# Three of the four tile pairs of an output projection by seven products, with the two up pairs behind it interleaved

## The chip, the cores and the metric

One core of a Trainium2 chip. The time is device time in microseconds from launch to end, the median of several runs; smaller is better. A profile of one execution stands beside it.

## The reference

One layer on a sequence of 1024 tokens of width 1024, all in float32. Cut to what matters here:

```python
z = rms_norm(h, norm_mix_g)
proj = z @ w_in                                    # 512 pool, 512 recurrent, 512 gate columns
y_pool = multiscale_pool_mixer(u_pool, ...)        # four groups of 128 channels
y_lru = rg_lru(conv(u_lru), ...) * gelu(u_gate)    # four groups of 128 channels
h = h + concatenate([y_pool, y_lru]) @ w_out       # the output projection, 1024 x 1024
z = rms_norm(h, norm_mlp_g)
h = h + square(relu(z @ w_up)) @ w_down            # 1024 -> 4096 -> 1024
h = h + sigmoid(rms_norm(h, norm_ple_g) @ w_ple_gate + b) * (p @ w_ple_proj)
return rms_norm(h, norm_final_g)
```

## The kernel before

Everything is kept with channels on the 128 partitions and the 1024 tokens along the row, so a tensor of width 1024 is eight tiles of 128 x 1024 (`H[0]` to `H[7]` for the residual stream). T[0] to T[5] are six more tiles of that size, R another; A and B are eight pairs each of operand tiles.

A float32 product is made of three products of rounded parts: `split` writes an upper part on ScalarE (a cast) and a lower part on VectorE (source less upper part), and `mm` multiplies upper by upper, upper by lower and lower by upper. Each TensorE instruction multiplies a 128 x 128 block of weights with 512 tokens.

The up and down projections already use seven products for eight (Strassen in Winograd's form): of a 2 x 2 arrangement of blocks, seven products P1 to P7 of sums of operands are made, and their sums give the four corners c11, c12, c21, c22. "Even" and "odd" tiles of a pair and the two halves of the tokens make the operand's 2 x 2; `up_operand` says which operand half each product uses. P1, P2 and P3 use halves as they are (raw), P4 to P7 use sums t1 to t4 made on VectorE. The weights' sums are made partly by accumulating DMAs (`grow`, issued by GpSimd, POOL in the profile), partly on VectorE, in `up_weight`, which also issues the loads of a later pair. An up pair's products can be accumulated onto a PSUM bank that another product or ScalarE wrote before.

The output projection is plain: for each of eight tiles `o`, eight input blocks `k` by three products by two halves of the tokens. `B[0]` to `B[3]` are the pooled channels (`pool_mix`), `B[4]` to `B[7]` the gated recurrent ones (`gate_out`). Of the first two tiles, blocks 0 to 5 come before 6 and 7, since those two are made last. Behind each tile the residual is added on VectorE (line 787), squares are summed for the norm (lines 403 and 404), and after each odd tile the four operand sums for the up projection are made and split into A (line 797 and the two splits behind it). Then `up_first` does the first up pair's seven products in an order of their own, and `up_pair` the others.

The order of the work: the kernel is written as one program, and a planner orders each engine's instructions by readiness and by priority (`tc.high_priority` raises it; `tc.issue_after` and `keep_in_program_order` hold instructions behind others). Each engine and each queue then runs its own list in order. Weights come through `weights()`: it asks for the next entry of the list `todo` and gives out the oldest that was asked for, so weights are split one or two entries ahead. Weight tiles live in four slots (`whi` and `wlo`, two each), raw weights in two (`raw`).

PSUM has eight banks: `pd` gives four single ones (`bank`), `pp` two double ones (`banks`).

Ahead of it all, the first loop (k = 0 to 7) loads the input tiles with the first weights on SP's queue and multiplies as they come; GpSimd computes a small series there (`softplus`, lines 498 to 509), whose result `cneg` and `cpos` the recurrence uses later (line 665).

## Time and profile before

| | us |
|---|---|
| median of 3 runs (918.67 to 919.38) | 919.19 |
| the profiled execution | 918.4 |
| its span, first to last instruction | 916.6 |
| TensorE busy in the span | 909.1 |
| VectorE busy | 703.8 |
| ScalarE busy | 468.6 |
| GpSimd busy | 38.9 |
| output projection on TensorE, 384 instructions | 82.88 |
| first up pair on TensorE, 84 instructions | 18.13 |

PE is TensorE's multiplication, PEld its weight load, DVE VectorE, ACT ScalarE, POOL GpSimd, SP the queue of plain loads and stores. A row of the timeline has its start, its length, engine, line, operation, what it writes and reads, and, in square brackets, how long the engine was idle before it and what ended that. Tile names leave out buffer numbers: `t_h` are the T and H tiles, `a` the A tiles, `y` the B tiles, `wu` and `wu_raw` raw up weights, `ps_o` the projection's banks.

### The profile page before, as it was taken

To read this page: it belongs to the slowest core of one execution; us is meant where nothing else is said; L and a number is where in the kernel's file an instruction comes from. 1 tells how busy PE (TensorE), PEld (TensorE's weight loads), DVE (VectorE), ACT (ScalarE), POOL (GpSimd) and SP (SyncE) were. 2 spreads that over 40 slices of the span, in tenths; PEclk is the share of its full clock that TensorE was granted. 3 is DMA by queue.
4 is the path that set the end of the run, shared out by engine and by line. 5 is a ranking of instruction groups with operands and counts; after the bars stand their busy time and mean duration, and the time that the engine had idled before them with its cause. 6 is when DMAs were issued, how large, how long until landed. Compare 5 with 4: busy or idle time off the path is not lost.

```text
span 916.6 us, 11225 instructions
## 1 busy us (share of the span) xinstructions
PE 909.1 (99%) x4225; PEld 792.0 (86%) x4225; DVE 703.8 (77%) x854; ACT 468.6 (51%) x606; POOL 38.9 (4%) x54
## 2 busy tenths in 40 slices
PE   9999999999999999999999999999999999999997
PEld 7888888888888888888888888888888888888886
DVE  7898984668986566656765899899876579799676
ACT  6558992447554454445444554344343446656223
POOL 4400001000000000000000000000000000000001
PEclk9999999999999999999999999999999999999999
DMA  7311055214377767876864987466633341031353
GB/s 274 102 46 46 24 182 140 81 46 117 103 209 224 210 163 217 227 197 169 231 206 164 353 335 276 131 195 203 201 117 117 115 162 46 1 119 67 92 174 136
DMA packets 56871, 142.46 MB, mean 155 GB/s; under 512 B 4977, under 2 KB 9969, under 8 KB 56817
## 3 DMA queue, kind: packets, MB, share of 16 engines
q1 hardware_dynamic: 54080, 132.84, 43.7%
q0 software_dynamic: 2736, 8.91, 5.7%
q8 instruction: 33, 0.54, 0.3%
q14 instruction: 22, 0.17, 0.1%
HBM read 106.08 MB, written 35.65 MB: 155 GB/s over the span
## 4 chain that ended last, share of the span: by engine, by line
PE 98%; issue 1%; DVE 0%; DVEq 0%; ACT 0%; POOLq 0%; POOL 0%
PE ps_P_d L363 32%; PE ps_b_u L363 12%; PE ps_i L363 9%; PE ps_o L363 9%; PE ps_d_u L363 8%; PE ps_a_u L363 8%; PE ps_e L363 8%; PE ps_l L363 3%; PE ps_P_u L363 3%; PE ps_e L1254 2%; PE ps_l L576 1%; PE ps_j L363 1%; PE ps_g L645 1%; PE ps_p L363 1%; PE ps_l_second L363 1%
## 5 line engine op out<-in xcount | busy, mean ns | idle before, releaser
L363 PE MATMUL ps_P_d<-a,wd_P_hi 128*128 128x512 f32 x880 | 261.7, 379 | 0.0
L363 PEld LDWEIGHTS ps_P_d<-a,wd_P_hi 128*128 128x128 f32 x880 | 166.3, 189 | 23.6
L363 PE MATMUL ps_P_d<-a,wd_P_lo 128*128 128x512 f32 x440 | 166.8, 379 | 0.0
L363 PE MATMUL ps_b_u<-a,wu_P 128*128 128x512 f32 x504 | 113.5, 379 | 0.0
L363 PEld LDWEIGHTS ps_b_u<-a,wu_P 128*128 128x128 f32 x504 | 95.3, 189 | 13.5
L363 PEld LDWEIGHTS ps_P_d<-a,wd_P_lo 128*128 128x128 f32 x440 | 83.2, 189 | 11.8
L363 PE MATMUL ps_a_u<-y,wu_P 128*128 128x512 f32 x360 | 82.6, 379 | 0.0
L363 PEld LDWEIGHTS ps_a_u<-y,wu_P 128*128 128x128 f32 x360 | 68.0, 189 | 9.7
L826 DVE TENSOR_TENSOR t_h<-t_h,ps_P_d 128x512 f32<-128x512 f32 (+1 forms) x56 | 42.5, 759 | 36.2 <-PE ps_P_d L363 36.2
L186 DVE TENSOR_TENSOR a<-wd,a 128x1024 fp32r<-128x1024 f32 x56 | 67.0, 1219 | 0.9 <-ACT a L185 0.6
L363 PE MATMUL ps_i<-a,wi_hi 128*128 128x512 f32 x256 | 66.1, 381 | 0.0
L363 PE MATMUL ps_o<-y,wo_hi 128*128 128x512 f32 x256 | 65.7, 379 | 0.0
L185 ACT ACTIVATE a<-wd 128x1024 fp32r<-128x1024 f32 x56 | 57.9, 1049 | 7.0 <-PE ps_P_d L363 7.0
L363 PEld LDWEIGHTS ps_i<-a,wi_hi 128*128 128x128 f32 x256 | 48.1, 189 | 8.0 <-issue 0.7
L363 PEld LDWEIGHTS ps_o<-y,wo_hi 128*128 128x128 f32 x256 | 48.4, 189 | 6.9
L185 ACT ACTIVATE wd_P_hi<-wd 128x1024 fp32r<-128x1024 f32 x24 | 25.3, 1055 | 56.0 <-PE ps_P_d L363 56.0
L844 DVE SCALAR_TENSOR_TENSOR t_h<-t_h,rstd 128x2048 f32<-128x2048 f32 x16 | 36.6, 2291 | 18.8 <-ACT t_h L863 18.8
L186 DVE TENSOR_TENSOR wu_P<-wu,wu_P 128x512 fp32r<-128x512 f32 x47 | 32.2, 687 | 21.8 <-ACT wu_P L185 21.8
L186 DVE TENSOR_TENSOR wu_P<-wu_raw,wu_P 128x512 fp32r<-128x512 f32 x45 | 30.9, 687 | 23.3 <-ACT wu_P L185 23.3
L363 PE MATMUL ps_d_u<-a,wu_P 128*128 128x512 f32 x180 | 41.3, 379 | 0.0
L363 PE MATMUL ps_d_u<-y,wu_P 128*128 128x512 f32 x180 | 41.3, 379 | 0.0
L185 ACT ACTIVATE wu_P<-wu 128x512 fp32r<-128x512 f32 x47 | 29.3, 625 | 21.1 <-PE ps_b_u L363 14.0
(267 smaller groups left out, 1545.7 us busy)
## 6 DMA issues: line engine op xcount, KB each, us to landing
wd<-act SPq DMA_DIRECT2D x56, 512.0 KB, 5.5
act<-t_h SPq DMA_DIRECT2D x32, 512.0 KB, 6.2
wu<-in_w_up SPq DMA_DIRECT2D x16, 512.0 KB, 4.7
act<-wu SPq DMA_DIRECT2D x16, 512.0 KB, 5.9
wd<-in_w_down SPq DMA_DIRECT2D x16, 512.0 KB, 5.8
wu_raw<-in_w_up SPq DMA_DIRECT2D x15, 512.0 KB, 5.5
t_h<-in_xT SPq DMA_DIRECT2D x14, 512.0 KB, 4.8
wg_raw<-in_w_gate SPq DMA_DIRECT2D x10, 512.0 KB, 3.3
```

The costliest lines, as they stand in the source:

```text
L185: first = pin(nc.scalar.activation(hi, src, AF.Copy))
L186: lowest[:] = [pin((eng or nc.vector).tensor_tensor(lo, src, f32(hi), ALU.subtract)).ins]
L363: ins = nc.tensor.matmul(ps, w, turns(z[:, hs]), start=first and z is zhi and w is whi, stop=last and w is wlo, skip_group_check=more,)
L576: nc.tensor.matmul(ps, kblk(w, o), turns(z[:, hs]), start=k == n == 0, stop=False)
L645: nc.tensor.matmul(x, w[r, o * P : (o + 1) * P], turns(z[r, at : at + HALF]), start=n == 0, stop=n == 2)
L826: (eng or nc.vector).tensor_tensor(to, to if y is None else y, x, ALU.add)
L844: nc.vector.scalar_tensor_tensor(cc, cc, 0.0, twice(R), ALU.max, ALU.mult)
L1254: nc.tensor.matmul(pg, z, turns(quad[x == 1][:, k]), start=n == 0, stop=n == 3 * NT - 1, skip_group_check=True)
```

## The change

The first two output tiles stay plain. The other three pairs (numbered -3, -2, -1 in the list of weights) are made by seven products each (`out_pair`), from operand sums of the mixed channels. `out_sums` makes these sums in place, in the tiles that hold the mixed channels, and splits them into A; to keep the tiles until then, the fourth gated tile goes to `H[6]`, two pooled tiles to `H[4]` and `H[5]`, and the other two are stored to HBM (`mixed`) and loaded back. The three raw products of a pair come first. P3's weight is the sum of all four blocks; for the three out pairs and the first two up pairs it is made in HBM by `sum_ahead`, called in the first loop: for each of five sums one copy and three accumulating transfers of 256 KB by GpSimd's queue. The corners of the first two such pairs are written over H, and the residual is added to them by an accumulating load; the last pair's are added to a residual loaded before.

The double PSUM banks are given up after the plain pair for four single ones (`part_upper`). The up operands' sums are in place too (`up_sums`, `up_even`, `up_odd`). The first two up pairs are interleaved (`up_two`), raw products first, with the norm's sums folded between them. In the last up pair P4 moves ahead of P2. The down stage keeps its products.

```diff
-    pp = ctx.enter_context(tc.tile_pool(name="pp", bufs=2, space=bass.MemoryType.PSUM))
     pd = ctx.enter_context(tc.tile_pool(name="pd", bufs=4, space=bass.MemoryType.PSUM))
+    upper_half = [ExitStack()]
+    pp = upper_half[0].enter_context(tc.tile_pool(name="pp", bufs=2, space=bass.MemoryType.PSUM))
+    pe = []
+    def part_upper():
+        upper_half[0].close()
+        pe.append(ctx.enter_context(tc.tile_pool(name="pe", bufs=4, space=bass.MemoryType.PSUM, reuse_waits="tile")))
...
+    def pair_source(m):
+        return w_up[m] if m >= 0 else w_pairs[m + NOUT]
+    def load_a22(m):
+        nc.sync.dma_start(up_raw[m]["P4"], pair_source(m)[:, A22])
+    full_sums = {m: dram.tile([P, HALF], F32, name=f"full{m}") for m in range(-NOUT, 2)}
+    out_raw = []
+    def sum_ahead():
+        for m, to in full_sums.items():
+            w = pair_source(m)
+            nc.gpsimd.dma_start(to, w[:, A21])
+            for x in (A22, A11, A12):
+                grow(to, w[:, x])
+    def load_pair(m):
+        w = pair_source(m)
+        a, c = (H[7], T[4]) if m == -2 else [raw_tile(f"wu{m}_{i}") for i in range(2)] if m % 2 else up_spare
+        (a11, a12), (chain, s3) = halved(a), halved(c)
+        a22, full = T[5][:, HALVES[m % 2]], chain if m < NPAIR - 1 else T[4][:, FIRST]
+        if m < 2:
+            few = {-3: out_raw[0], -2: R, -1: T[5]}.get(m, out_raw[1])
+            full = few[:, HALVES[int(m == 1)]]
+            if m < 0:
+                a22 = few[:, SECOND]
+        up_raw[m] = {"P1": a11, "P2": a12, "P4": a22, "P5": chain, "P6": chain, "P7": s3, "P3": full}
         nc.sync.dma_start(a, w[:, A11.start : A12.stop])
         if m < 2:
+            nc.sync.dma_start(full, full_sums[m])
             load_a22(m)
+        nc.sync.dma_start(both(c), twice(w[:, A21]))
+        grow(c, w[:, : 2 * HALF])
...
+    RAW_FIRST = "P1", "P3", "P2", "P5", "P6", "P4", "P7"
+    UP = [(m, kind) for m in range(-NOUT, 0) for kind in RAW_FIRST]
+    UP += [(m, kind) for kind in RAW_FIRST[:3] for m in TWO]
+    UP += [(0, "P5"), (0, "P6"), (1, "P5"), (0, "P7"), (1, "P6"), (0, "P4"), (1, "P7")]
+    for m in range(2, NPAIR - 1):
+        UP += [(m, "P1"), (m, "P5"), (m - 1, "P4"), (m, "P6"), (m, "P2"), (m, "P3"), (m, "P7")]
     m = NPAIR - 1
+    UP += [(m, "P1"), (m, "P5"), (m - 1, "P4"), (m, "P4"), (m, "P2"), (m, "P3"), (m, "P6"), (m, "P7")]
     def up_weight(m, kind):
+        raw, last = up_raw[m], m == NPAIR - 1
         w = wp.tile([P, S], F32R, tag=next(up_place), name=f"wu{m}_{kind}")
         hi, lo = (w[:, hs] for hs in HALVES)
+        with tc.high_priority(URGENT) if m < 0 else ExitStack():
+            split(raw[kind], hi, lo)
+            if kind == "P5":
+                dv(ALU.add, raw["P5"], raw["P5"], raw["P1"])
+                if last:
+                    dv(ALU.add, raw["P3"], raw["P6"], raw["P2"])
+            elif kind == "P6" and 2 <= m < NPAIR - 1:
+                dv(ALU.add, raw["P3"], raw["P6"], raw["P2"])
+        if kind == "P7" and m < NPAIR - 2 and m != -2:
+            load_pair(m + 2)
+        if kind == "P4" and 0 <= m < NPAIR - 2:
+            load_a22(m + 2)
         return hi, lo
...
         if k == 3:
             tables()
+            sum_ahead()
...
-    GATED = T[5], T[1], T[0], T[1]
+    GATED = T[5], T[1], T[0], H[6]
+    MIXED = T[5], T[2], H[4], H[5]
...
+            if pair == 0:
+                nc.sync.dma_start(mixed[:, t], y)
...
-    out_w, out_ps = {}, {}
-    for o in range(NT):
-        nc.sync.dma_start(H[o], xT[o * P : (o + 1) * P, :])
-        if o == 0:
-            out_w = {0: weights(), 1: asked.pop(0)}
-            seed_up()
-            for i in range(2):
-                out_ps[i] = psum(f"ps_o{i}")
-                out_parts(i, out_w[i], out_ps[i], range(NT - 2))
-        elif o == 1:
-            ask()
-        else:
-            out_w[o], out_ps[o] = weights(), psum(f"ps_o{o}")
-        out_parts(o, out_w[o], out_ps[o], range(NT - 2, NT) if o < 2 else range(NT))
-        ps = out_ps[o]
-        z = T[o % 2]
-        end = o == NT - 1
-        for hs, part in ps:
-            hv = by(H[o][:, hs], part)
-            nc.vector.tensor_tensor(hv, hv, got(part), ALU.add)
-            if end:
-                nc.scalar.activation(z[:, hs], H[o][:, hs], AF.Identity, scale=col("g_mlp", o))
-        if not end:
-            norm.add(H[o])
-            nc.scalar.activation(z, H[o], AF.Identity, scale=col("g_mlp", o))
-        if o % 2 == 1:
-            z11, z12, z21, z22 = (T[i][:, hs] for i in range(2) for hs in HALVES)
-            t2, t3, t4, t1 = (T[i][:, hs] for i in (2, 3) for hs in HALVES)
-            for to, x, y in ((t1, z11, z12), (t2, z22, t1), (t3, z12, z22), (t4, z21, t2)):
-                nc.vector.tensor_tensor(to, x, y, ALU.add if to is t2 else ALU.subtract)
-            split(T[2], *A[o // 2])
-            split(T[3], *A[4 + o // 2])
...
+    def out_operand(kind, t):
+        if kind in ("P5", "P7"):
+            return half(A[t], int(kind == "P7"))
+        if kind in ("P4", "P6"):
+            return half(A[4 + t], int(kind == "P6"))
+        return half(B[2 * t + (kind != "P1")], int(kind == "P3"))
...
+        if t == 3 and kind in ("P1", "P2", "P3", "P4"):
+            return half(A[3 + int(kind[1])], 0)
+        if kind == "P4":
+            return half(B[2 * t], 1)
+        return out_operand(kind, t)
...
+    def seed(b, a):
+        nc.scalar.activation(b, a, AF.Copy, scale=-1.0)
+    def sums(even, odd):
+        (z11, z12), (z21, z22) = halved(even), halved(odd)
+        dv(ALU.subtract, z11, z11, z12)
+        dv(ALU.subtract, z12, z12, z22)
+        dv(ALU.add, z22, z22, z11)
+        dv(ALU.subtract, z21, z21, z22)
+    def out_sums(t, even, odd):
+        sums(even, odd)
+        split(even, *A[t])
+        split(odd, *A[4 + t])
+    def residual(o):
+        return xT[o * P : (o + 1) * P, :]
+    def first_out(i):
+        ps = out_ps[i]
+        for hs, part in ps:
+            add_got(H[i][:, hs], part)
+    for o in range(2):
+        nc.sync.dma_start(H[o], residual(o))
+    out_w = [weights(), asked.pop(0)]
+    leave("hl")
+    out_raw += space("hr", 2, F32, waits="tile")
+    load_pair(-NOUT)
+    load_pair(-2)
+    out_ps = [[(slice(0, S), banks(f"ps_o{i}"))] for i in range(2)]
+    for ks in (range(NT - 2), range(NT - 2, NT)):
+        for i in range(2):
+            out_parts(i, out_w[i], out_ps[i], ks)
+    for _ in range(2):
+        ask()
+    for t in range(2):
+        nc.sync.dma_start(T[2 + t], mixed[:, t])
+    out_sums(2, T[5], T[1])
+    out_sums(1, H[4], H[5])
+    out_sums(0, T[2], T[3])
+    with tc.high_priority(URGENT):
+        for i in range(2):
+            first_out(i)
+    part_upper()
+    out_sums(3, T[0], H[6])
+    def corners(q):
+        return [H[2 * q + i][:, hs] for i in range(2) for hs in HALVES]
+    def out_pair(q, end=False):
+        m = q - 1 - NOUT
+        c11, c12, c21, c22 = corners(q)
+        keep = add_got if end else copy
+        a, d = bank(f"ps_a_o{q}"), bank(f"ps_d_o{q}")
+        b, f = upper_bank(f"ps_b_o{q}"), upper_bank(f"ps_f_o{q}")
+        pair_product(m, "P1", a)
+        seed(b, a)
+        pair_product(m, "P3", d)
+        keep(c22, d)
+        pair_product(m, "P2", a, more=True)
+        keep(c11, a)
+        yield "raw"
+        pair_product(m, "P5", d, more=True)
+        if end:
+            add_got(c12, d)
+        pair_product(m, "P6", b, more=True)
+        if end:
+            less(c12, b)
+        else:
+            copy(c12, b)
+            take(c12, d, c12)
+        pair_product(m, "P4", f)
+        keep(c21, f)
+        yield "fourth"
+        pair_product(m, "P7", b, more=True)
+        add_both(both(H[2 * q + 1]), b)
+        less(c22, d)
+        if not end:
+            for o in (2 * q, 2 * q + 1):
+                grow(H[o], residual(o))
+    def up_raw_part(t, kinds):
+        for kind in kinds:
+            o = 2 * t + (kind != "P1")
+            split(H[o][:, HALVES[kind == "P3"]], *up_operand(kind, t), col("g_mlp", o))
+    def up_sums(t, even, odd):
+        for i, z in enumerate((even, odd)):
+            nc.scalar.activation(z, H[2 * t + i], AF.Identity, scale=col("g_mlp", 2 * t + i))
+        sums(even, odd)
+    def up_odd(t, odd):
+        split(odd[:, FIRST], *up_operand("P4", t))
+        split(odd[:, SECOND], *up_operand("P6", t))
+    def up_even(t, even):
+        split(even, *A[t])
+    for q in (1, 2):
+        for _ in out_pair(q):
+            pass
+        up_sums(q - 1, T[2 * q - 2], T[2 * q - 1])
+    norm = Norm("n1", R, T[4:5])
+    for o in range(4):
+        norm.add(H[o])
+    for o in (6, 7):
+        nc.sync.dma_start(H[o], residual(o))
+    stages = out_pair(3, True)
+    next(stages)
+    leave("y2")
+    *E, u0, u1 = space("wu", 4, F32, "right", "tile")
+    up_spare += u0, u1
+    load_pair(0)
+    for t in range(3):
+        up_raw_part(t, RAW_FIRST[:3])
+    next(stages)
+    up_raw_part(3, RAW_FIRST[:1])
+    up_sums(2, *E)
+    for _ in stages:
+        pass
+    up_raw_part(3, RAW_FIRST[1:3])
+    for t in range(2):
+        up_even(t, T[2 * t])
+        up_odd(t, T[2 * t + 1])
+    up_sums(3, T[0], T[1])
+    up_even(2, E[0])
+    up_odd(2, E[1])
+    up_even(3, T[0])
+    up_odd(3, T[1])
+    for o in range(4, NT):
+        norm.add(H[o])
...
+    def up_two():
+        (a, d), (b, f) = ([[new(f"ps_{x}_u{m}") for m in TWO] for x in xs] for new, xs in ((bank, "ad"), (upper_bank, "bf")))
+        cc = [corner_sums(m)[1:] for m in TWO]
+        for m in TWO:
+            pair_product(m, "P1", a[m])
+            seed(b[m], a[m])
+        for m in TWO:
+            pair_product(m, "P3", d[m])
+        for m in TWO:
+            pair_product(m, "P2", a[m], more=True)
+            copy(cc[m][0], a[m])
+        leave("hr")
+        small[:] = space("hl", 2, F32R, waits="tile")
+        for hs in HALVES:
+            norm.fold(hs, T[4][:, hs])
+        def fifth(m):
+            pair_product(m, "P5", f[m])
+            copy(cc[m][3], f[m])
+        def sixth(m):
+            c12 = cc[m][1]
+            pair_product(m, "P6", b[m], more=True)
+            copy(c12, b[m])
+            take(c12, d[m], c12)
+            add_got(c12, f[m])
+        def seventh(m):
+            pair_product(m, "P7", b[m], more=True)
+            take(cc[m][3], b[m], cc[m][3])
+        fifth(0)
+        sixth(0)
+        norm.rstd(R, [x for hs in HALVES for x in norm.folded(hs)])
+        fifth(1)
+        seventh(0)
+        sixth(1)
+        chains[0] = b[0]
+        up_fourth(0)()
+        seventh(1)
+        chains[1] = b[1]
+        leave("hl")
...
+        ps = mlp_bank(f"ps_P4_u{m}")
+        pair_product(m, "P4", ps)
+        copy(c21, ps)
...
+        W[0, 3] = raw_tile("w11_3")
+        load_w(0, 0, 3)
...
-            ps = banks(f"ps_e{g}_{o}")
-            pair = ps[:, :HALF], ps[:, HALF:]
+            pair = upper_bank(f"ps_e{g}_{o}"), upper_bank(f"ps_j{g}_{o}")
...
+    wo = np.asarray(w_out)[0].reshape(NT // 2, 2, P, NT // 2, 2, P).transpose(3, 4, 1, 2, 0, 5)
+    wo = np.stack([wo[1:, i, j] for i, j in ((1, 1), (0, 0), (0, 1), (1, 0))], axis=2)
```

210 lines of the change are left out of this document (59 added, 151 removed).

## The prediction

> **What bounds the kernel now.** I read the page first, then the chain of waits in order of time.
>
> ```profile
> span 916.6 us, 11225 instructions
> PE 909.1 (99%) x4225; PEld 792.0 (86%) x4225; DVE 703.8 (77%) x854; ACT 468.6 (51%) x606; POOL 38.9 (4%) x54
> PE 98%; issue 1%; DVE 0%; DVEq 0%; ACT 0%; POOLq 0%; POOL 0%
> ```
>
> ```profile
> 120.99 20.72 PE ps_i L363 x96
> 141.71 82.88 PE ps_o L363 x384
> 224.59 18.13 PE ps_P_u L363 x84
> 242.72 2.59 PE ps_a_u L363 x12
> ```
>
> TensorE is the chain. Each piece begins where the last one ended (141.71 + 82.88 = 224.59), so there is no gap around the change: whatever removes a matmul is gained whole, and whatever makes TensorE wait is lost whole. So the next question is what cover the other engines have. The view by stretches gives it; its columns are the stretch and its length, then busy time of PE, PEld, DVE, ACT, POOL, the granted clock, DMA share and GB/s.
>
> ```profile
> 2.00:16.00 14.00, 14.00 (x60) 10.85 (x59) 10.47 (x22) 8.65 (x17) 2.70 (x7) 1.00 0.95 337
> 121.00:141.70 20.70, 20.70 (x97) 18.12 (x97) 19.81 (x18) 16.21 (x17) 0.00 (x0) 1.00 0.55 200
> 141.70:159.90 18.20, 18.20 (x87) 15.92 (x86) 6.02 (x7) 4.38 (x5) 2.74 (x3) 1.00 0.61 149
> 141.70:253.10 111.40, 111.40 (x518) 97.55 (x517) 77.57 (x101) 56.20 (x71) 5.43 (x6) 1.00 0.36 96
> ```
>
> VectorE is full ahead of the output projection (19.81 of 20.70), two thirds idle in its first 18.2 us (6.02), and has 77.57 of 111.4 over the stretch that the new projection and the first two up pairs will fill.
>
> **The change part by part.**
>
> *Matmuls.* One matmul is 82.88 / 384 = 0.2158 us. A pair of output tiles takes 96 now (two tiles, eight blocks, three products, two halves) and 7 × 4 × 3 = 84 by seven products. Three pairs: 36 fewer, **-7.77 us**. The up pairs keep 84 each (18.13 us), the down stage keeps its count. TensorE would then have the plain pair from 141.71 to 162.43, three raw products to 170.2, the third pair's end at 216.8 and two up pairs to 253.1, if nothing waits.
>
> *VectorE's prices.* The nearest rows, from the timeline:
>
> ```profile
> 159.87 1.22 DVE L787 TENSOR_TENSOR t_h<-t_h,ps_o 128x1024 f32<-128x1024 f32 x1 [10.11 <-PE ps_o L363]
> 166.48 1.89 DVE L797 TENSOR_TENSOR t_h<-t_h 128x512 f32<-128x512 f32 x3
> 168.89 2.36 DVE L186 TENSOR_TENSOR a<-t_h,a 128x1024 fp32r<-128x1024 f32 x2 [0.52 <-ACT a L185]
> 218.94 6.04 DVE L189 SCALAR_TENSOR_TENSOR y<-t_h,y 128x512 fp32r<-128x512 f32 x9
> 238.15 1.29 DVE L445 TENSOR_TENSOR t_h<-t_h 64x512 f32<-64x512 f32 x2
> 239.36 0.94 DVE L448 CAST hl<-t_h 64x512 fp32r<-64x512 f32 x2
> 240.34 1.59 DVE L449 TENSOR_TENSOR hl<-t_h,hl 64x512 fp32r<-64x512 f32 x2
> 250.01 1.31 DVE L465 STREAM_TRANSPOSE rstd<-n_ps 128x512 f32<-128x512 f32 x2
> 252.04 0.47 DVE L470 RECIPROCAL edge<-edge 128x16 f32<-128x16 f32 x2
> 252.43 1.24 DVE L471 STREAM_TRANSPOSE rstd<-edge 128x512 f32<-128x512 f32 x2
> 254.16 2.28 DVE L844 SCALAR_TENSOR_TENSOR t_h<-t_h,rstd 128x2048 f32<-128x2048 f32 x1
> ```
>
> So a half row (512) is 0.63, a full row (1024) 1.18, a scaled half 0.67.
>
> *New sums before the projection (out_sums).* Four calls of four half sums and two full lower parts: 4 × (2.52 + 2.36) = 19.5 us on VectorE, none there before. They are due at the first product that isn't raw: P5 of the first pair, 170.2, its fourth block at 172.1; the last lower part (1.18) only in P6. By 159.9 VectorE has 18.2 - 6.0 = 12.2 us for them. From there to 172.1 it must also do first_out (2 × 1.18), five lower weight halves and one chain sum (6 × 0.63), 6.2 in all, which leaves 6.0. Due 18.3, room 18.2: the margin is nil. Lower bound 0. Upper bound: only the long idle piece of 10.11 is used and each call waits 0.52 for ScalarE, so 2.1 + 2.1 = 4.2. I take **+0.5**, near the lower end, since the P4 weight can slip behind them.
>
> *Weight halves, and how far ahead.* Each out weight is now a half tile in one of four slots. The first needs the slot of the first plain tile.
>
> ```profile
> 159.49 1.06 ACT L185 ACTIVATE wo_hi<-wo_raw 128x1024 fp32r<-128x1024 f32 x1 [10.99 <-PE ps_o L363]
> 213.83 0.63 ACT L185 ACTIVATE wu_P<-rstd 128x512 fp32r<-128x512 f32 x1 [3.21 <-PE ps_o L363]
> 245.34 0.58 ACT L926 ACTIVATE ps_b_u<-ps_a_u 128x512 f32<-128x512 f32 x1 [0.23 <-PE ps_a_u L363]
> ```
>
> The kernel before makes the same jump with a whole tile (1.06 + 1.22 from 159.49, used at 162.43) and TensorE doesn't wait; half tiles need 0.63 + 0.63. Cost 0, covered by the plain pair's last 2.6 us. ScalarE's new work (21 half casts less 6 whole, 8 whole casts for the sums, some 13 PSUM copies and seeds at 0.58) is about 23 us, 79 of 111.4: no bound.
>
> *The rest of the stretch.* VectorE from 141.7 to 253.1: what stays of the recurrence 6.0; out_sums 19.5; first_out 2.4; 21 weight halves and 3 chain sums 15.1; the pairs' corners 2 × 2.44 + 4.96 = 9.9; the up operands 10.1 + 4.7 + 5.0 + 8.0 = 27.8; the norm 7 × 1.18 + 3.8 + 3.0 = 15.1; two up pairs 22 × 0.63 = 13.9; the first finish_up 4.7. Sum 114.4 against 111.4 us. So VectorE goes from 70% to full. But norm and finish_up (19.8) don't feed the next products: they may slide behind 253, where a pair leaves it slack, and 94.6 fit. What is late next is the norm's two small matmuls, which the code puts after eight of the two up pairs' fourteen products, at 237.5. Bounds 0 and 4 (3.0 us of excess and the 1.2 of a full row ahead of it); I take **+0.2**.
>
> *Loads that are moved.* The accumulating loads of each pair go out on POOL (0.86 each) behind all that stands there before.
>
> ```profile
> 0.72 0.10 POOL L502 MEMSET sp<- 128x4 f32 x1 [0.29 <-POOLq L1493]
> 3.75 0.24 POOL L513 TENSOR_TENSOR sp<-t_h 128x4 f32<-128x4 f32 x1 [2.93 <-DMA t_h<-in_w_vec_x]
> 12.91 0.24 POOL L498 TENSOR_SCALAR sp<-sp 128x4 f32<-128x4 f32 x1 [8.93 <-ACT sp L497]
> 32.41 1.83 POOL L509 TENSOR_SCALAR sp<-sp 128x4 f32<-128x4 f32 x1
> 159.13 0.86 POOL L227 DMA_DIRECT2D rstd<-in_w_up x1 [5.19 <-DMA rstd<-in_w_up]
> ```
>
> ```profile
> q0 software_dynamic: 432, 0.79, 31.6%
> ...
> rstd<-in_w_up POOLq DMA_DIRECT2D x3, 256.0 KB, 5.0
> ```
>
> The second fence is the DMA view from 150 to 166 us: three accumulating transfers of 256 KB, 5.0 us each to land, 31.6% of 16 us, so 1.69 us of all DMA engines each. sum_ahead adds 20 of that size (5 copies, 15 that accumulate) from HBM to HBM; each sum waits for the one before, so POOL is held about 5.9 us a step, up to 118 us. The first pair's own chain is needed at 170 and would be free of this at about 150.
>
> Where they start matters more. The planner puts on POOL what is ready: L502 and L513 ran ahead of L498, which precedes them in the code. The twenty transfers wait for nothing, so they may begin at about 1 us, in the stretch where the DMA engines are full (0.95 from 2 to 16 us). The tightest load there:
>
> ```profile
> 15.42 1.15 ACT L188 ACTIVATE a<-t_h 128x1024 fp32r<-128x1024 f32 x1 [0.19 <-DMA t_h<-in_xT]
> 17.09 1.20 DVE L189 SCALAR_TENSOR_TENSOR a<-t_h,a 128x1024 fp32r<-128x1024 f32 x1
> 21.25 1.03 PE L363 MATMUL ps_l<-a,wl_hi 128*128 128x512 f32 x4
> ```
>
> The fifth input tile lands at 15.4, its lower part is done at 18.3, TensorE needs it at 21.25: 2.96 us to spare. One transfer at a time takes 1.69 of 5.9 us, 29% of the DMA engines; the loads from 2 to 15.4 then stretch by 1/0.71, 5.4 late, and TensorE waits 2.4. With half of the engines taken they are 13.4 late and it waits 10.4. With a later start it is 0. Bounds 0 and 10.4; I take **+1.0**, between none and one at a time.
>
> [...]
>
> *At no cost:* storing and reloading two pooled tiles (512 KB each; due at 160, DMA share 0.61 then), the residual by accumulating loads (two for each of two pairs, due only when the up operands are made, a pair later), four single PSUM banks in place of two pairs, and the new order in the last up pair. Each has a whole pair (18.1 us) or the idle half of the DMA engines as cover; without it a late load costs its 5 to 8 us.
>
> *Sum.* 918.4 (the profiled execution) - 7.77 + 0.5 + 0.2 + 1.0 = 912.3. The median of the runs stands 0.8 above the profiled execution, so **913.1**.
>
> **The rivals.**
>
> *VectorE becomes the bound at the sums.* For it: margin nil at 172.1, 114.4 us of work in 111.4. Against: a sixth of that can slide. Price 4.2 + 4 at most, half of it likely: one wait of about 4 us, 915.6. [...]
>
> *The start slowed a little:* one transfer at a time throughout, 2.4 in place of 1.0, with the small waits 914.5.
>
> *Slower: the ahead-sums flood the start.* Place: 2 to 16 us, DMA queues. Price by the share taken: a half gives 10.4 of waiting against 7.77, 918.4 + 2.6 + 0.8 = 921.8. It decides from 45% on (10.7 late = 7.77 + 2.96, over 13.4 + 10.7). For it: five of the twenty don't depend on each other and could be in flight together; the engines are full then. Against: POOL waits in order for each sum. The same queue also holds the softplus steps, done at 34.2 and used at 82.5; eight of the twenty put ahead of them (8 × 5.9) use that room up.
>
> *The products aren't removed,* or come back elsewhere: the counts of the code say no; I give it nothing.
>
> **How the numbers follow.** Forecast (911.2 to 914) 0.53; VectorE the bound 0.16; start a little slowed 0.17; flooded start 0.12; POOL's softplus late 0.02. Faster or slower by 0.2% means below 917.4 or above 921.0, about what a measurement of this kernel can tell from no change. The forecast lies below; of the VectorE case 0.14 does, of the small start case 0.13 (more than one transfer at a time for the rest); 0.05 of the flooded start stays within, 0.07 and the softplus case lie above. So faster 0.80, same 0.11, slower 0.09. The range runs from all terms at 0 (911.4, less 0.4 of scatter) to 918.5, which leaves out the flooded start and the worst of the others.
>
> **What would show it.** 36 fewer matmuls, the projection's four pieces 20.7 and three times 18.1 us. A wait of TensorE on a lower part of "a" near 172 is the sums' price, one ahead of the norm's small matmuls near 240 the slide's; TensorE idle before 36 us with ScalarE waiting for x is the start's, with POOL's transfers issued in the first microseconds. The prediction is wrong if TensorE waits somewhere not named here, or if its pieces aren't 0.2158 us a matmul.

## The result, and the profile after

The changed kernel takes 949.93 us (median of 4 runs, 947.08 to 952.24); the kernel before took 919.10 beside it. The ratio is 1.0334, with a 95% interval of 1.0306 to 1.0363: 31 us slower, where 6 us faster was forecast. The profiled execution took 952.24 us, with a span of 950.5 beside 916.6.

The page of the changed kernel, its first lines and its chain by engine:

```profile
span 950.5 us, 11308 instructions
PE 914.9 (96%) x4189; PEld 790.4 (83%) x4189; DVE 732.7 (77%) x900; ACT 490.7 (52%) x646; POOL 51.8 (5%) x78
PE 71%; DVE 15%; DMA 7%; ACT 3%; issue 3%; SPq 0%; DVEq 0%; POOLq 0%; POOL 0%; ACTq 0%
```

The 36 matmuls are gone (4225 to 4189). Yet TensorE, which was 98% of the chain, is 71% of it, and it is busy for longer. At the mean of before (909.1 / 4225), 4189 matmuls last 901.3 us, so 13.6 us of the 914.9 are matmuls that ran slowly. Idle time went from 7.5 to 35.6 us, 28.1 more. The sum is 28.1 + 13.6 - 7.8 = 33.9, the difference of the spans.

Where it is lost shows in the pieces of TensorE. The timeline of the changed kernel, at the start of the projection, the three places where it stood still longest behind it, and the first up product:

```profile
153.11 1.03 PE L384 MATMUL ps_o<-y,wo_hi 128*128 128x512 f32 x4
...
178.89 5.49 PE L384 MATMUL ps_a_o<-y,wu-3_P 128*128 128x512 f32 x12 [4.54 <-ACT wu-3_P L196]
...
207.57 4.38 PE L384 MATMUL ps_a_o<-y,wu-2_P 128*128 128x512 f32 x12 [2.18 <-ACT ps_b_o L843]
...
244.01 2.11 PE L384 MATMUL ps_a_u<-y,wu_P 128*128 128x512 f32 x9
...
260.27 3.28 PE L384 MATMUL ps_d_u<-y,wu_P 128*128 128x512 f32 x7 [5.83 <-DVE wu_P L197]
```

The projection starts 11.4 us late (153.11 where before had 141.71, both by the same product). It lasts 90.9 us to the first up product, where 384 less 36 matmuls would be 75.1: 15.8 lost. From there to the end of P6 of the third up pair, the seventeenth up product in both kernels, before needed 44.5 us (224.59 to 269.05) and the changed kernel 57.4 (244.01 to 301.36): 12.9 lost. The chain of waits has the product behind these two ends, first of the kernel before, then of the changed one:

```profile
269.05 2.59 PE ps_a_u L363 x12
```

```profile
301.36 2.59 PE ps_a_u L384 x12
```

The rest adds 1.6. So these three stretches lose 40 us, of which the removed matmuls pay for 7.8. The view of stretches of the changed kernel, with the columns of the prediction:

```profile
2.00:16.00 14.00, 9.70 (x33) 6.69 (x32) 6.04 (x13) 2.90 (x9) 3.58 (x7) 0.88 0.97 302
150.00:170.00 20.00, 19.92 (x93) 17.13 (x92) 20.00 (x24) 10.44 (x11) 1.76 (x2) 1.00 0.60 166
178.00:185.00 7.00, 6.11 (x15) 4.87 (x16) 6.43 (x10) 5.18 (x9) 0.00 (x0) 0.51 0.22 75
240.00:260.00 20.00, 10.88 (x44) 8.20 (x44) 20.00 (x28) 14.65 (x22) 1.73 (x2) 0.83 0.32 62
```

*The start.* From 2 to 16 us TensorE has 9.70 of 14.00 where it had 14.00. The timeline of POOL in the changed kernel, and the DMA view of its first 50 us:

```profile
1.30 0.75 POOL L261 DMA_DIRECT2D full-3_136<-in_w_pairs  x1 [0.47 <-issue]
2.03 0.58 POOL L261 DMA_DIRECT2D full-2_137<-in_w_pairs  x1
2.58 0.54 POOL L261 DMA_DIRECT2D full-1_138<-in_w_pairs  x1
3.10 0.54 POOL L261 DMA_DIRECT2D full<-in_w_up  x1
```

```profile
q0 software_dynamic: 2128, 4.46, 46.5%
q1 hardware_dynamic: 3227, 7.76, 45.9%
...
t_h<-in_xT SPq DMA_DIRECT2D x6, 512.0 KB, 10.2
```

Four of the five copies go out together in the first four microseconds. GpSimd's queue q0 takes 46.5% of the DMA engines, and the input tiles land 10.2 us after their issue. The same view of the kernel before has no q0 and 5.8 us:

```profile
q1 hardware_dynamic: 3456, 8.56, 49.4%
...
t_h<-in_xT SPq DMA_DIRECT2D x6, 512.0 KB, 5.8
```

*The projection's start.* Behind the wait of 4.54 us stand twelve matmuls that took 5.49 us in place of 2.59, and the stretch from 178 to 185 has a granted clock of 0.51. What the wait is for is in the timeline of ScalarE:

```profile
177.25 1.06 ACT L196 ACTIVATE a<-t_h 128x1024 fp32r<-128x1024 f32 x1 [2.48 <-DVE t_h L229]
178.22 0.61 ACT L196 ACTIVATE wu-3_P<-wu-3_0_raw 128x512 fp32r<-128x512 f32 x1
...
205.88 1.15 ACT L933 ACTIVATE t_h<-t_h 128x1024 f32<-128x1024 f32 x1 [5.00 <-DMA t_h<-in_xT]
206.94 0.58 ACT L843 ACTIVATE ps_b_o<-ps_a_o 128x512 f32<-128x512 f32 x1
```

The cast of the first weight, 0.61 us, stands on ScalarE behind a cast of `out_sums` that had waited 2.48 us for VectorE, which is full there (20.00 of 20 us from 150 to 170). No raw product needs that sum.

*The second pair.* In the same fence a scaling of the up sums waits 5.00 us for the accumulating residual load, and the seed of the next pair's chain (ScalarE's copy of that pair's first product, with its sign turned, into the bank that later products are added onto) stands behind it. That is the wait of 2.18 us at 207.57. One pair later a square of the norm waits 3.37 us for such a load, again ahead of the seed, and TensorE waits 1.68.

*The up pairs' start.* TensorE waits from 254.4 to 260.27 for a lower part, one of the two in the second row of this fence from VectorE's timeline:

```profile
255.45 0.70 DVE L229 TENSOR_TENSOR t_h<-t_h 128x512 f32<-128x512 f32 x1
...
259.52 1.30 DVE L197 TENSOR_TENSOR wu_P<-hr,wu_P 128x512 fp32r<-128x512 f32 x2
```

VectorE does not rest from 240 to 260 (20.00 of 20). Ahead of the two subtractions of 0.65 us stand an addition of the norm and operand sums such as the first row's and their lower parts, which the first product of sums (ps_f_u, at 270.68 in the chain of waits) needs 10 us later.

### The profile page after: what moved, and what is told of

Same layout as the page of the kernel before. It is cut to its first block, busy times and chain, and to the rows that moved or that the text cites. A ratio compares the mean times of both kernels' runs of the same rounds, so it can differ in the third digit from the quotient of the medians.

```text
span 950.5 us, 11308 instructions
## 1 busy us (share of the span) xinstructions
PE 914.9 (96%) x4189; PEld 790.4 (83%) x4189; DVE 732.7 (77%) x900; ACT 490.7 (52%) x646; POOL 51.8 (5%) x78
## 4 chain that ended last, share of the span: by engine, by line
PE 71%; DVE 15%; DMA 7%; ACT 3%; issue 3%; SPq 0%; DVEq 0%; POOLq 0%; POOL 0%; ACTq 0%
PE ps_P_d L384 31%; PE ps_b_u L384 11%; PE ps_d_u L384 8%; PE ps_a_u L384 8%; PE ps_e L384 7%; DMA t_h<-in_xT 3%; PE ps_e L1379 2%; PE ps_j L384 2%; DVE t_h L229 2%; DMA wu<-in_w_up 1%; DVE a L197 1%; DVE t_h L640 1%; DVE y L197 1%; DVE t_h L627 1%; DMA wl_raw<-in_w_lru 1%
## 5 line engine op out<-in xcount | busy, mean ns | idle before, releaser
L384 PE MATMUL ps_b_u<-a,wu_P 128*128 128x512 f32 x405 | 92.3, 379 | 0.0
L384 PEld LDWEIGHTS ps_b_u<-a,wu_P 128*128 128x128 f32 x405 | 76.5, 189 | 10.9
L384 PE MATMUL ps_a_u<-y,wu_P 128*128 128x512 f32 x288 | 68.3, 382 | 2.0 <-ACT wu_P L196 2.0
L384 PEld LDWEIGHTS ps_a_u<-y,wu_P 128*128 128x128 f32 x288 | 54.5, 190 | 10.2 <-ACT wu_P L196 2.6
L229 DVE TENSOR_TENSOR t_h<-t_h 128x512 f32<-128x512 f32 x46 | 31.5, 690 | 33.8 <-ACT t_h L991 23.6
L384 PE MATMUL ps_d_u<-a,wu_P 128*128 128x512 f32 x216 | 51.5, 379 | 0.0
L384 PEld LDWEIGHTS ps_d_u<-a,wu_P 128*128 128x128 f32 x216 | 41.0, 190 | 5.9
L384 PE MATMUL ps_d_u<-y,wu_P 128*128 128x512 f32 x144 | 35.7, 393 | 6.1 <-DVE wu_P L197 5.8
```

The source lines that it names most:

```text
L229: return nc.vector.tensor_tensor(to, x, y, op).ins
L384: ins = nc.tensor.matmul(ps, w, turns(z[:, hs]), start=first and z is zhi and w is whi, stop=last and w is wlo, skip_group_check=more,)
```

## The experiments

Differences below are of medians; each kernel also has its ratio to the kernel before, with its 95% interval.

**The twenty transfers alone, in the kernel before.**

```diff
+    full_sums = {m: dram.tile([P, HALF], F32, name=f"full{m}") for m in range(5)}
+    def sum_ahead():
+        for m, to in full_sums.items():
+            nc.gpsimd.dma_start(to, w_up[m][:, A21])
+            for x in (A22, A11, A12):
+                grow(to, w_up[m][:, x])
...
+            sum_ahead()
```

> The kernel before with only the twenty ahead-sum transfers added (same size, same sources of 256 KB, into buffers that nothing reads), called at the same place of the first loop; the computation is unchanged. Theory 'flooded start': between before and after, the first input-gate product ps_i starts at 46.88 and at 58.29 us, 11.4 us later, and the twenty transfers alone make this. Expected: 930.5 us (919.1 + 11.4), ps_i near 58, GpSimd's softplus ending near 50 in place of 34. Rival 'the start is late for another reason' (other weights' layout, the planner's other choices): within 2 us of 919.1 and ps_i near 47.

Measured: 928.35 us, ratio 1.0103 (1.0088 to 1.0118). The chain of waits of this kernel:

```profile
2.11 8.81 DMA wl_raw<-in_w_lru
...
55.66 10.36 PE ps_i L372 x48
```

The first gate product starts at 55.66 where before had 46.88, 8.8 late. So the transfers alone cost 9.2 us; the flooded start is shown. The changed kernel's 11.4 has 2 us more, and no run parts those.

**The transfers held behind the softplus series**, in the changed kernel.

```diff
+        series_end.append(nc.gpsimd.tensor_scalar_mul(cneg, cpos, -1.0).ins)
...
-            sum_ahead()
+            with tc.issue_after(series_end[0]):
+                sum_ahead()
```

> The changed kernel with the twenty ahead-sum transfers held behind the last step of the softplus series on GpSimd (done near 34 us when it is undisturbed), same computation. Theory 'flooded start': TensorE gets back the 11.4 us of the start and the rest is as in after: 949.9 - 11.4 = 938.5 us, ps_i starts near 47. Rival: the transfers only move their harm, for they are then in the way of the loads from 34 to 110 us: between 940 and 950, with new waits of TensorE on casts of loaded tiles in that stretch.

Measured: 940.67, ratio 1.0235 (1.0220 to 1.0250): 9.3 us back, 2.1 less than expected. TensorE is busy for all of 2 to 36 us again, and its first gate product starts at 47.05 in the timeline (46.72 before). The time itself lies in the rival's range (940 to 950), but its sign is missing: TensorE waits nowhere from 34 to 110 us. The 2.1 us are lost later, where the waits for seeds grew from 3.9 to 5.4 us in all and the one for a lower part from 5.8 to 6.4. The next ones build on this kernel.

**ScalarE's scalings behind the next pair's fourth product.**

```diff
+        with tc.issue_after(marks["fourth", q]):
             up_sums(q - 1, T[2 * q - 2], T[2 * q - 1])
...
+    with tc.issue_after(marks["fourth", 2]):
         for o in range(4):
             norm.add(H[o])
```

> As the one with the ahead-sums held back, and beside it ScalarE's scalings of the up sums (which wait for the accumulating residual transfers, 5.00 and 3.37 us of ScalarE standing still in after) are put behind the next pair's fourth product's copy, and with them the squares of the norm; the computation is the same. Theory 'order on ScalarE': the seeds of the second and third output pair no longer stand behind them, so the waits ahead of wu-2 (2.18 us and 1.79 of half clock) and wu-1 (1.68) go, about 5 us: near 933.5 beside 938.5. Rival 'VectorE is the bound': it is 100% busy from 150 to 170 and from 240 to 260 us in after, and work put later only adds to the second stretch: within 1.5 us of the kernel it is made from, or slower.

Measured: 938.35, ratio 1.0209 (1.0192 to 1.0226), 2.3 us back in place of 5. The waits of TensorE in this kernel (us in total, times, longest) begin with

```profile
PE ps_d_u L384 <- DVE wu_P L197: 10.9, 1, 10.9
PE ps_a_o L384 <- ACT wu-3_P L196: 4.5, 1, 4.5
```

The run also holds the casts of raw operands of the first up products, and the norm's last squares, behind the third pair's seed. Both waits for seeds are gone, and half of what they gave is lost again at the up pairs' start, where the wait for a lower part grew from 6.4 to 10.9 us. Each theory has half of it.

**The last call of `out_sums` behind the first weight.**

```diff
-    out_sums(3, T[0], H[6])
+    with tc.issue_after(first_up), tc.issue_after(first_low):
+        out_sums(3, T[0], H[6])
```

> As the one with the ahead-sums held back, and beside it the last of the four calls that make the projection's operand sums is held behind the first product's weight parts (both its upper part on ScalarE and its lower part on VectorE); the computation is the same. Theory 'order on ScalarE': in after wu-3_P's cast (178.22, 0.61) stood behind casts of sums (2.48 us of waiting for VectorE) that the raw products don't need; with fewer of them ahead, the wait of 4.54 us and the 2.9 us of half clock behind it (twelve matmuls in 5.49 in place of 2.59) shrink by 2 to 7 us: 931 to 936 beside 938.5. Rival 'VectorE is the bound': the sums come later by what the weights come earlier, TensorE waits for the last sum's lower part at the first product of sums in place of it, and the time stays within 1.5 us.

Measured: 936.81, ratio 1.0195 (1.0180 to 1.0210), 3.9 us back: within the 2 to 7 us of "order", though not within its 931 to 936, which counted from 938.5 in place of 940.67. The timeline has, in place of a wait of 4.54 and a halved clock:

```profile
165.40 2.43 PE L384 MATMUL ps_a_o<-y,wu-3_P 128*128 128x512 f32 x10 [1.71 <-DVE wu-3_P L197]
```

**High priority for the first up pairs' weights.**

```diff
-        with tc.high_priority(URGENT) if m < 0 else ExitStack():
+        with tc.high_priority(URGENT) if m < 2 else ExitStack():
```

> As the kernel with the ahead-sums held back (940.7), and beside it the planner's high priority for weight parts, which the output pairs have, is given to the first two up pairs too; the computation is the same. In that kernel TensorE waits 6.4 us for the lower part of an up weight on VectorE, which stands behind some 20 us of operand sums that only later products need, and 2.0 for an upper part on ScalarE; twenty matmuls behind the wait take 6.56 us in place of 4.32. Theory 'order on VectorE': the weights' lower parts (0.68 each) go ahead, the waits fall to 2 us in all: 931 to 934. Rival 'VectorE is too full there (18.84 of 20 us from 240 to 260)': the operands of the later products become late by the same amount, and TensorE waits for a lower part of them instead: within 2 of 940.7.

Measured: 933.98, ratio 1.0160 (1.0141 to 1.0179), 6.7 us back. The wait of 6.4 us for a lower part of an up weight is gone from the list, and 1.2 us at the norm's small matmuls is the longest wait left at the up pairs. The operand sums that stood ahead were not needed yet: order, not the amount of work, made this wait.

**The three changes of order at once.**

> The ahead-sums held back, and all three changes of order at once: ScalarE's scalings behind the fourth product's copy (alone 940.7 to 938.4), the last operand sum behind the first weight (to 936.8), the up weights at high priority. The computation is the same. Theory 'order': the gains are at different places and add: -2.3 - 3.9 - 8 = 926.5, slower than before by 7 us, since the accumulating residual loads (7 us to land) stay. Rival 'VectorE is the bound over the whole of the stretch': the stretch has about 114 us of its work in 104, and whatever is moved shows up as a wait elsewhere: not below 933.

Measured: 927.86, ratio 1.0092 (1.0077 to 1.0107). Together they give 12.8 us, the sum of the three (2.3 + 3.9 + 6.7 = 12.9), as "order" had it; the rival's 933 is passed. The longest waits left are 3.2 us for a seed and 1.9 for an operand's lower part, both at the up pairs.

**The residual loaded first**, with the last sum behind the first weight and the weights at high priority, without the held scalings.

```diff
     for q in (1, 2):
-        for _ in out_pair(q):
+        for o in (2 * q, 2 * q + 1):
+            nc.sync.dma_start(H[o], residual(o))
+        for _ in out_pair(q, True):
             pass
```

> The ahead-sums held back, the last operand sum behind the first weight, the up weights at high priority, and the residual of the second and third output pair loaded on SP ahead of their products and added to the PSUM parts on VectorE (as the last pair does), in place of copies on ScalarE and four accumulating transfers afterwards. The result is the same sum. Theory 'late residual': the seeds no longer stand behind scalings that wait for a transfer (4.06 and 1.35 us of waiting in the kernel with the sums ordered, and 1.9 of half clock behind the first): 936.8 - 8 (weights) - 7.3 = 921.5, though VectorE has 4 x 0.68 more for each pair. Rival 'VectorE is the bound': those 5.4 us come on top: 930 or more, the waits on lower parts grow.

Measured: 920.66, ratio 1.0019 (1.0009 to 1.0028). It has VectorE do more (735.0 us by its page, 732.7 in the changed kernel) and is 7.2 us faster than the three orders, near the forecast of "late residual" (921.5). It differs from them in three things: no accumulating transfers, eight corner copies fewer on ScalarE, and nothing held. Against the two orders that it keeps, which would give 930.1 if their gains add (an estimate: 940.67 - 3.9 - 6.7), it gives 9.4. So making the residual late cost 7 to 9 us; how much of that is the transfers and how much the copies no run parts.

**Operand sums early, their parts behind the first weight.**

```diff
-    out_sums(0, T[2], T[3])
+    sums(T[2], T[3])
...
+    sums(T[0], H[6])
+    with tc.issue_after(first_up), tc.issue_after(first_low):
+        for t, even, odd in ((0, T[2], T[3]), (3, T[0], H[6])):
+            split(even, *A[t])
+            split(odd, *A[4 + t])
```

> As the one with the residual loaded first, but of the projection's operand sums two calls are parted: the sums themselves are made as early as before, only their upper and lower parts are held behind the first weight of the projection. Same computation. Theory 'order on ScalarE': the cast of the first weight no longer waits for VectorE's sums (in the kernel with one call held it starts at 162.26, behind a cast that waited 2.41 us, and TensorE waits 1.71 us): 1 to 2 us less than the one it is made from. Rival: the lower parts that were moved are due at the first product of sums (ps_d_o at 172.8) and are late there by what the weights gained: no difference, within 0.7.

Measured: 920.16, ratio 1.0016 (1.0007 to 1.0026): 0.5 less, which these runs can't tell from none, as the rival had it. The waits of TensorE in this kernel and three of its stretches:

```profile
PE ps_d_o L384 <- DVE t_h L823: 1.2, 1, 1.2
PE n_ps L478 <- DVE hl L470: 1.2, 1, 1.2
PE ps_P_d L384 <- ACT a L196: 1.1, 1, 1.1
PE ps_a_o L384 <- DVE wu-3_P L197: 0.9, 1, 0.9
```

```profile
133.00:150.00 17.00, 17.00 (x81) 14.88 (x80) 17.00 (x19) 10.61 (x12) 0.90 (x1) 1.00 0.76 221
150.00:160.00 10.00, 9.95 (x47) 8.39 (x46) 10.00 (x13) 3.71 (x5) 0.86 (x1) 1.00 0.83 256
220.00:240.00 20.00, 19.39 (x89) 16.35 (x88) 20.00 (x29) 14.37 (x23) 0.00 (x0) 1.00 0.37 81
```

What is left are waits of about 1 us, three of the four for VectorE, which is full in all three stretches; the waits come behind them (163 to 174, and 253 us). The granted clock is 1.00 again.

**The old order of the last up pair, three fine changes of order, and both.** The first puts P4 of the last pair behind P2 and P3 again, in the list of weights and in `up_last`; the second has three edits:

```diff
-    UP += [(m, "P1"), (m, "P5"), (m - 1, "P4"), (m, "P4"), (m, "P2"), (m, "P3"), (m, "P6"), (m, "P7")]
+    UP += [(m, "P1"), (m, "P5"), (m - 1, "P4"), (m, "P2"), (m, "P3"), (m, "P4"), (m, "P6"), (m, "P7")]
```

```diff
-    with tc.high_priority(URGENT):
+    with tc.high_priority(URGENT), tc.issue_after(first_low):
         for i in range(2):
             first_out(i)
...
-        keep(c22, d)
+        with tc.high_priority(URGENT):
+            keep(c22, d)
...
-        norm.rstd(R, [x for hs in HALVES for x in norm.folded(hs)])
         fifth(1)
         seventh(0)
+        norm.rstd(R, [x for hs in HALVES for x in norm.folded(hs)])
```

> As the kernel whose operand sums are parted (920.2), and beside it the last up pair's products stand in the order of the kernel before again (P2 and P3 ahead of its own P4). The computation is the same. In that kernel the first down products wait 1.07 us for an upper part and 0.56 for a lower part; the chain of waits shows a load of 5.93 us into the tiles of the raw operands, released by the last raw product at 508.72. Theory 'the new order of the last pair delays the loads': two raw products one product earlier (2.59 us) take both waits away: -1.6, 918.5. Rival 'the order costs nothing': within 0.5.

> As the kernel whose operand sums are parted (920.2), and beside it three small changes of order: the first pair's residual additions go behind the first weight's lower part (TensorE waits 0.89 us there), the copy of the corner that P5 accumulates onto goes at high priority (1.20), and the norm's two small matmuls go behind two more products (1.16). The computation is the same. Theory 'order': 3.2 us in all, 917.0. Rival 'VectorE is full' (20.00 of 20 us from 220 to 240): the waits move to other lower parts and half or less is gained: 918.5 or more.

> The three small changes of order and the old order of the last pair together; the computation is the same. If both theories hold: 920.2 - 1.6 - 3.2 = 915.4, faster than before (919.0) by 3.6. If VectorE is the bound in the stretch: 917 to 918.5.

Measured: 920.74, ratio 1.0022 (1.0013 to 1.0032), for the last pair; 919.36, ratio 1.0005 (0.9996 to 1.0014), for the fine order; 919.25, ratio 1.0009 (1.0000 to 1.0017), for both. The old order of the last pair gains nothing (0.6 us slower than without it): that rival holds. The two together miss both of their forecasts (915.4, and 917 to 918.5). Of the fine order's 3.2 us no more than 0.8 came, and the waits of TensorE in that kernel show how:

```profile
PE ps_a_o L384 <- ACT ps_b_o L846: 1.3, 1, 1.3
PE n_ps L478 <- DVE hl L470: 1.2, 1, 1.2
```

The waits of 0.9 and 1.2 at the first pair are gone, and one of 1.3 for its seed stands there. The norm's matmuls wait as before: the planner did not move them with the code.

**GpSimd takes work from VectorE**: the norm's last four additions, the four sums of the pooled tiles, or both.

```diff
+    norm.eng = nc.gpsimd
     for o in range(4, NT):
         norm.add(H[o])
...
-    sums(T[2], T[3])
+    sums(T[2], T[3], nc.gpsimd)
```

> As the kernel with the three fine changes of order (919.4), and the last four additions of the norm's squares (128 x 1024, 1.22 us each on VectorE) are made on GpSimd; the computation is the same. No row shows such an addition on GpSimd, which stands idle there. Theory 'VectorE is what is left of the loss': VectorE has 4.9 us less from 239 to 250, and the waits there (0.60 for a lower part, 1.16 for the norm's small matmuls, 0.24 for a subtraction) shrink: 917.5 to 918.5 if GpSimd needs less than 2.5 us each. Rival 'GpSimd is slower than VectorE there, and its time stands on the path of the norm': TensorE waits longer for the small matmuls, 921 or more.

> As the kernel with the three fine changes of order (919.4), and the four half sums of the two pooled tiles ahead of the projection (128 x 512, 0.68 us each on VectorE) are made on GpSimd; the computation is the same. Theory 'VectorE is what is left of the loss': it is busy 17 of 17 us from 133 to 150 and 10 of 10 from 150 to 160, so 2.7 us less takes away the wait of 1.28 us at the first output pair: 918. Rival 'GpSimd is too slow': four sums one behind the other at over 3 us each come after 170, and TensorE waits for the first product of sums: 921 or more.

> Both on GpSimd, the computation is the same. If VectorE is what is left of the loss: 916.5 to 917.5, faster than before (919.0). If GpSimd's own time decides: slower than 920.

Measured: 929.47, ratio 1.0112 (1.0096 to 1.0127); 921.35, ratio 1.0030 (1.0018 to 1.0041); 931.53, ratio 1.0132 (1.0118 to 1.0145). All three are slower. In the first, an addition took 2.38 to 8.47 us on GpSimd, and ScalarE stood still behind it for 5.51 us. In the second GpSimd made its four sums from 121 to 137 us, about 2 us each in place of 0.68, and VectorE slowed beside them, from 6.97 to 10.16 us for the same instructions (last section). So they took nothing from VectorE, and as tests of whether it is the bound they are inconclusive.

**VectorE's work left out.**

```diff
-    sums(T[2], T[3])
...
-    sums(T[0], H[6])
...
-    for o in range(4, NT):
+    for o in ():
         norm.add(H[o])
```

> As the kernel with the three fine changes of order (919.4), with VectorE's work cut: two of the four calls of half sums ahead of the projection (eight of 0.68 us) and the last four squares and additions of the norm (1.22 us each on VectorE) are left out, so the operands and the norm are not the reference's. Theory 'VectorE is what is left of the loss': with 5.4 us less ahead of the projection and 4.9 less behind it the waits listed there (1.28, 0.60, 1.16, 0.24) and the small ones beside them go: 915 or less. Rival 'what is left lies elsewhere (the start, the order of TensorE's own list, the last pair)': within 1 of 919.4.

Measured: 915.58, ratio 0.9960 (0.9947 to 0.9972), 3.8 us less than with the work. Four squares on ScalarE went with the additions (485.8 to 481.0 us busy). Of the waits of 1.28, 0.60, 1.16 and 0.24 us, 0.3 and 0.3 are left in the list of waits, beside a new one:

```profile
PE ps_b_o L384 <- DVE t_h L839: 1.4, 1, 1.4
```

The forecast of "VectorE" (915 or less) is missed by 0.6, and that of "elsewhere" (within 1 of 919.4) by 2.8. What was left out is worth about half of what is left: 919.36 less the 911.4 of all removed matmuls is 8.0, and this run gives back 3.8. It is nearly all VectorE's work, but ScalarE's squares and the casts that waited for the sums are in it too.

**Work moved from VectorE to ScalarE and the transfers**, first at the first seven-product pair, then at the plain pair (in both the scalings that need the residual are held; the second also puts the seeds at high priority):

```diff
-        for _ in out_pair(q, True):
+        for _ in out_pair(q, q == 2):
             pass
```

```diff
-            add_got(H[i][:, hs], part)
+            copy(H[i][:, hs], part)
+        grow(H[i], residual(i))
```

> As the kernel with the three fine changes of order (919.4), but the first output pair has its residual by accumulating transfers again and copies on ScalarE (2.5 us less on VectorE between 165 and 187, where TensorE waited 1.28), and the first two up sums' scalings are held behind the second pair's fourth weight, so that no seed stands behind them. The result is the same sum. If VectorE ahead of the first pair's corners is a part of what is left: 917.5 to 918.5. If not, or if the later up sums fall into the full stretch behind 220 (20.00 of 20 us): 919.4 to 921.

> As the kernel with the three fine changes of order (919.4), but the plain pair's parts are copied out of PSUM on ScalarE and get their residual by two accumulating transfers (VectorE 2 x 1.21 us less behind 162, where the first pair's corners, seed and operand sums are late), the scalings that need this residual are held behind the first pair's weights, and the seeds go at high priority. The result is the same sum. Cutting 10 us of VectorE's work gave 3.8 us; theory 'VectorE is half of what is left': 2.4 us less at the place of the 1.28 us wait gives 1.0 to 1.5: 918.0 to 918.5. Rival 'late residual', as with the first pair's (923.9): the scalings wait for the transfers and hold ScalarE: 921 or more.

Measured: 923.90, ratio 1.0055 (1.0041 to 1.0069), and 919.16, ratio 1.0003 (0.9994 to 1.0012). The first is 4.5 us slower, beyond both of its forecasts; it makes a residual late again. The second is the same as without it, between its two forecasts. No version that computes the reference was faster than before; the best, the fine order and the one with the plain pair copied, stand at its time.

## Why the prediction was wrong

The step that failed is the pricing of waits: four terms were put at or near nothing, and the runs gave back 9.3 us for the moved loads, 3.9 for the weight halves, 6.7 for the rest of the stretch and 7 to 9 for the residual. The slower rival that was named, the flooded start, is 11 of the 37 us between forecast and result; the others are mostly waits for weights and seeds, places that the prediction did not name, and by its own last sentence that makes it wrong.

**Matmuls, -7.77: right.** 36 are gone, and where nothing waits a product still takes 2.59 us for twelve. The sentence that whatever makes TensorE wait is lost whole was too mild: beside and behind the waits the matmuls also took longer, by 13.6 us in all, some 10 of them at half clock (below).

**Loads moved, +1.0: the wrong value from the right bounds.** 11.4 us were lost at the start, 9.2 of them by the transfers alone. The step's upper bound was 10.4 at half of the DMA engines, and q0 took 46.5%. I argued for few at a time because POOL waits in order for each sum; but the first four are copies that wait for nothing, and behind them four chains of sums ran side by side. The price of one transfer was about right: 46.5% of 50 us for 4.46 MB is 1.37 us of all DMA engines for 256 KB, where the row that I priced it by had 1.69. The flooded start was named, with its place, its price and its point of decision (45%), and 0.12 was too little for it. Softplus ended at 49.6 in place of 34.2, and no wait of TensorE is for it.

**Weight halves at cost 0: wrong.** The cover named, the plain pair's last 2.6 us, was there; the raw weight was too. What failed is "how far ahead", taken from the durations alone: the cast of 0.61 us stood in ScalarE's list behind casts that waited for VectorE (the last of them 2.48 us). That is the wait of 4.54 us and the 2.9 behind it. Holding one call of sums gave 3.9 back.

**out_sums, +0.5 with margin nil: the place was wrong.** VectorE was full from 150 to 170, as a margin of nil says, but TensorE waited for no lower part of "a" at P5. It waited at the first raw product, for a weight that stood behind the sums in ScalarE's queue; so no run shows this term's own size.

**The residual by accumulating loads at no cost: wrong.** They are due only when the up operands are made, a pair later, as written. But the scaling that uses them stands in ScalarE's list ahead of the next pair's seed, and ScalarE stood still ahead of the two for 5.00 us at the second pair. At the third a square of the norm stood there, and ScalarE waited 3.37 us. With the residual loaded first and added on VectorE, and the scalings no longer held, the kernel is 7.2 us faster (927.86 to 920.66).

**The rest of the stretch, +0.2: wrong by its assumption that what can slide will slide.** The norm and the operand sums did not slide; weights did, behind them. In the changed kernel VectorE was busy for 90.7 of the 111.4 us from the projection's start (153.1 to 264.5), so it was full in places only. With the order mended it is busy for 107.2 of 111.4 (the fine order, 142.5 to 253.9), and there the forecast of a full VectorE is nearly right. Priority for the weights alone gave 6.7 back. The rival that makes VectorE the bound holds for about half of the last 8 us, not for the 31.

**The order in the last pair and the PSUM banks at no cost:** the first holds (no gain from the old order), the second no run tested by itself.

**The granted clock** has no term in the forecast's sum. It reads 1.00 in every stretch of the kernel before that the prediction lists, and 0.51 from 178 to 185 us in the changed kernel. Up to that kernel's last matmul it is 0.50 from 10.76, 38.07, 178.02, 208.74 and 253.11 us on, which are 8, 41, 9 and 13 times 3.41 us apart, and each time for one, two or three times 3.41 us. The length of one wait does not tell where. These are stretches of that length ahead of the half clock and at it, first of the changed kernel (the wait of 2.18 us), then of the first pair's late residual (two waits of 0.84 and 1.22 us); the last line is of the kernel with GpSimd's sums (a wait of 2.0 us, and no half clock behind it):

```profile
205.32:208.74 3.42, 1.24 (x6) 1.05 (x6) 1.33 (x3) 2.86 (x5) 0.00 (x0) 1.00 1.00 200
208.74:212.15 3.41, 3.41 (x9) 2.70 (x8) 0.76 (x3) 1.62 (x3) 0.00 (x0) 0.50 0.25 50
258.36:261.77 3.41, 1.68 (x7) 1.28 (x8) 3.32 (x7) 0.32 (x1) 0.00 (x0) 1.00 0.43 119
261.77:265.18 3.41, 3.41 (x10) 2.69 (x9) 3.41 (x9) 0.95 (x2) 0.00 (x0) 0.50 0.00 0
168.88:172.29 3.41, 1.47 (x7) 0.94 (x5) 2.35 (x4) 3.02 (x5) 0.00 (x0) 1.00 0.00 0
```

In the changed kernel, cut into stretches of 3.41 us from its first record of the clock to the last matmul, TensorE was busy for at most 1.24 us in the stretch ahead of each half clock, and for 1.85 us or more in every other one at full clock. Between the two the lines above stand on both sides: 1.68 us with half clock behind it, 1.47 us without. What sets the clock no run shows. In the changed kernel TensorE is busy for 19.8 us at half clock, and half of that, 9.9 us, is what the clock cost (an estimate). The other 3.7 of the 13.6 come without it: the kernel with the operand sums parted, whose clock is 1.00, still has 904.2 us of matmuls where 901.3 were expected.

**What stays open.** With the order mended the kernel stands at 919.4, 8.0 above what the removed matmuls promise. Its profiled span is that of the kernel before, 916.6 us: idle time is 11.6 in place of 7.5 us, and the matmuls take 905.0 where 901.3 were expected, at a granted clock of 1.00. So it is lost in many short stops and in longer matmuls. The work left out, nearly all VectorE's, gives back 3.8; 0.8 is the start, where the first gate product of that kernel is at 47.51 in the timeline (46.72 before). The rest no run settles.

## What to carry to other kernels

A cost of nothing needs two covers: time in which the work could be done, and a place in its engine's list where nothing slow stands ahead of it. Before a change is priced, ask of every instruction that it adds what that instruction waits for, and which short instruction that feeds the bound will stand behind it; four of the five transfers here that wait for nothing were issued between 1.30 and 3.64 us. Where TensorE may wait, price slow matmuls behind the wait as well: beside 28.1 us more of idle time, the changed kernel has matmuls that took 13.6 us longer.

## What the runs showed of the hardware

VectorE's instructions took longer here while GpSimd made its sums. The timeline of VectorE with GpSimd idle (the fine order), and with GpSimd making its sums at the same time, and GpSimd's own:

```profile
132.05 2.28 DVE L702 TENSOR_TENSOR_SCAN t_h<-t_h 128x1024 f32<-128x1024 f32 x1
134.25 1.20 DVE L711 TENSOR_TENSOR t_h<-t_h 128x1024 f32<-128x1024 f32 x1
135.37 3.49 DVE L197 TENSOR_TENSOR y<-t_h,y 128x1024 fp32r<-128x1024 f32 x3
```

```profile
130.58 3.38 DVE L702 TENSOR_TENSOR_SCAN t_h<-t_h 128x1024 f32<-128x1024 f32 x1
133.88 2.22 DVE L711 TENSOR_TENSOR t_h<-t_h 128x1024 f32<-128x1024 f32 x1
136.03 4.56 DVE L197 TENSOR_TENSOR y<-t_h,y 128x1024 fp32r<-128x1024 f32 x3
```

```profile
130.26 6.97 POOL L855 TENSOR_TENSOR t_h<-t_h 128x512 f32<-128x512 f32 x3 [8.01 <-DMA t_h<-mixed]
```

The same instructions last 10.16 in place of 6.97 us: 3.2 more, where the four sums that GpSimd took are 2.7 us on VectorE. Why, no run shows.

The granted clock was the other surprise: behind two waits of 0.84 and 1.22 us it read 0.50, and behind one of 2.0 us it stayed at 1.00.
